# Seven-product blocks in all four feed-forward stages, and a changed supply of their weights

## The chip, the cores and the metric

The kernel runs on one NeuronCore of a Trainium2 chip, as one program. The metric is the device time of one execution in microseconds. The engines are TensorE (PE, with its weight loads PEld), VectorE (DVE), ScalarE (ACT), GpSimd (POOL) and SyncE (SP), which issues all DMAs of the kernel before.

## The reference

A sequence of 512 tokens with 1024 channels, all in fp32, goes through two blocks. The first has two layers; each is a feed-forward stage, a token mixing (three kinds of attention) and a second feed-forward stage, so there are four of these (`D_FF` is 2816):

```python
def swiglu(h, w_gate, w_up, w_down):
    return (jax.nn.silu(h @ w_gate) * (h @ w_up)) @ w_down
...
for l in range(DEPTH):
    x = x + 0.5 * swiglu(rmsnorm(x, ffn1_norm[l]), ffn1_w_gate[l], ffn1_w_up[l], ffn1_w_down[l])
    x = x + token_mixing(rmsnorm(x, mix_norm[l]), ...)
    x = x + 0.5 * swiglu(rmsnorm(x, ffn2_norm[l]), ffn2_w_gate[l], ffn2_w_up[l], ffn2_w_down[l])
```

The second block projects the normed x with one wide matrix, runs a state-space scan (S5) and a gated recurrence (RG-LRU) over the sequence, and merges the two.

## The kernel before, in words

**Layout.** Activations are held transposed: `xt[m]`, m from 0 to 7, is [128 channels, 512 tokens]. To keep fp32 accuracy each matmul operand is split into a high part in fp32r and a low part, the rest; `mm3` (L170) makes three matmuls, high by high, high by low and low by high. `wload` (L155) fetches a weight tile of up to [128, 1024] to a raw tile (tag `raw`, three buffers) by a DMA on SP's queue. For each piece of 512 columns ScalarE copies the high part (L164) and VectorE subtracts for the low part (L165), into the tags `whi` and `wlo`, four buffers each. `split` (L175) does the same for other operands.

**Stages 0 and 3, `ffn` (L227).** The 2816 hidden features are 22 rows of 128. A row needs two weight tiles, gate and up, of 24 matmuls with 512 columns each; I call each of these a row tile. Eleven rows are made, then their down products (L257) into the eight `xt[m]`; then the other eleven. A hook runs one step of side work for each row: `positions` (L420) in stage 0 makes the attention's bias tables and the rotary angles, `prepare` (L1001) in stage 3 makes block 2's constant operands. Both are generators, and most of their steps are VectorE work with some DMA writes. `prepare` also has transposes and small matmuls for each of its four parts.

**Stages 1 and 2, `ffn_blocks` (L319).** The first four rows (`NCLS` pairs) are row tiles as above. While they run, `blocks` (L330) norms x and makes from pairs of x tiles, halved in tokens, the seven operands of a Strassen-Winograd product; four are sums, kept in `ts` and split into `xh` and `xl` after the fourth row. Then each of nine pairs of rows makes two block problems, gate and up, with `gate_up` (L275): two raw tiles are fetched, VectorE makes four sums (L284 to L287), seven [128, 512] operands are split into pieces (ring of 8 from `whi` and `wlo`, and `NFX` = 12 from `fx`), and seven products of 12 matmuls with 256 columns accumulate in PSUM. ScalarE copies (L304, L306, L308) and VectorE adds (L310 to L315) take results out between them, where the next product goes on in the same bank:

```python
product(y, "a11", "b11", True)
act(c1[:, L], y, AF.Copy)
product(z, "s1", "t1", True)
act(c2[:, R], z, AF.Copy)
product(y, "s2", "t2", False)
act(c1[:, R], y, AF.Copy)
```

A problem has 84 matmuls with 256 columns in the place of two row tiles with 48 of 512. The pairs stand in groups, `FGRP` (L50), of 8, 8 and 6 rows, each followed by its down products (L406).

**Block 2, `block2` (L1158).** Its middle part runs four streams (L1384): the scan `s5`, the recurrence `lru`, the gates, and a final norm. Steps are interleaved by a list of due times. All of its projections fetch weights through `wload`, 32 tiles of 1024 columns and ten of 256 (L1301) in the streams. POOL has products of its own there (L1231, L1309, L1326).

**What sets the order.** The program is written in one order; a list scheduler then orders each engine's instructions by that order's priority and its estimate of when operands and buffers come free. An instruction may so run ahead of earlier ones on its engine if its buffers are free. A tile in a closed pool's space waits for the tiles that lay there.

Of the kernel before, what the change touches and what calls it, by code (L numbers as in the profile page):

```python
# [17 lines left out]
P = 128  # L18
# [31 lines left out]
FGRP = ((0, 8), (8, 16), (16, 22))  # L50
NCLS = 2
NFX = 12
BLOCKS = (1, 2)
# [46 lines left out]
def body(tc, A, out, tap, upto=99):  # L100
# [7 lines left out]
    with ctx:  # L108
# [45 lines left out]

        def wload(src, n):  # L155
# [71 lines left out]
        def ffn(i, nxt, pre, hook=None):  # L227
            with tc.tile_pool(name=f"fp{i}", bufs=1, reuse_waits="tile") as fp:
                for hf in range(2):
                    hh, hl = [], []  # L230
                    for f in range(NH):
                        ff = hf * NH + f
                        if hook is not None and ff >= 1:
                            if ff == 1:
                                work = hook(fp)
                            next(work, None)
                        gp = psum("pg")
                        up = psum("pu")
                        for j, o in ((0, gp), (1, up)):
                            wh, wl = ahead if i == ff == j == 0 else wload(A[f"gu{i}"][ff, :, j, :], KD * P)  # L240
                            for k in range(KD):
                                c = slice(k * P, (k + 1) * P)
                                mm3(o, wh[:, c], wl[:, c], xh[KORD[k]], xl[KORD[k]], k == 0, k == KD - 1)
                            if ff == 0:
                                next(pre)
                        t = tmp("t")
                        u = tmp("u")
                        V.tensor_tensor(t, gp, rstd, op=ALU.mult)
                        act(t, t, AF.Silu)
                        V.tensor_tensor(u, up, rstd, op=ALU.mult)  # L250
                        V.tensor_tensor(u, u, t, op=ALU.mult)
                        a = fp.tile([P, S], F32R, tag="h", name="hh", bufs=2 * NH)
                        b = fp.tile([P, S], F32R, tag="h", name="hl", bufs=2 * NH)
                        split(a, b, u)
                        hh.append(a)
                        hl.append(b)
                    for m in range(KD):  # L257
                        o = psum("pd")
                        for k0, k1 in ((0, 6), (6, NH)):
                            wh, wl = wload(A[f"dn{i}"][m][:, (hf * NH + k0) * P:(hf * NH + k1) * P], (k1 - k0) * P)  # L260
                            for k in range(k0, k1):
                                c = slice((k - k0) * P, (k - k0 + 1) * P)
                                mm3(o, wh[:, c], wl[:, c], hh[k], hl[k], k == 0, k == NH - 1)
                        V.scalar_tensor_tensor(out=xt[m], in0=o, scalar=0.5, in1=xt[m], op0=ALU.mult, op1=ALU.add)
                        if hf == 1 and nxt is not None:
                            nxt.tile(m)

# [7 lines left out]
        def gate_up(p, j, xk, fp, turn):  # L275

            rows = []
            for f in (2 * p, 2 * p + 1):
                r = wp.tile([P, WMAX], F32, tag="raw", name="raw", bufs=NRAW)
# [9 lines left out]
            for n, w in (("a11", a11), ("s1", s1), ("s2", s2), ("s4", s4), ("s3", s3), ("a12", a12), ("a22", a22)):  # L289
                ws[n] = piece(fp, turn), piece(fp, turn)  # L290
                split(*ws[n], w)
# [14 lines left out]
            act(c2[:, R], z, AF.Copy)  # L306
            product(y, "s2", "t2", False)
            act(c1[:, R], y, AF.Copy)  # L308
            product(z, "s4", "b22", False)
            V.tensor_tensor(c1[:, R], z, c1[:, R], op=ALU.add)  # L310
            product(y, "s3", "t3", False)
            V.tensor_tensor(c2[:, R], y, c2[:, R], op=ALU.add)
            x = psum("sx")[:, L]
            product(x, "a12", "b21", True)
            V.tensor_tensor(c1[:, L], x, c1[:, L], op=ALU.add)  # L315
            product(y, "a22", "t4", False)
            return c1, c2, y

        def ffn_blocks(i, nxt, pre):  # L319
            with tc.tile_pool(name=f"fp{i}", bufs=1, reuse_waits="tile") as fp:  # L320
                def htile(name, dt=F32R):
                    return fp.tile([P, S], dt, tag="h", name=name, bufs=16)
# [5 lines left out]
                ts = []  # L328

                def blocks(q):  # L330
                    xn = []
                    for m in (2 * q, 2 * q + 1):
                        t = htile("xn", F32)
                        V.scalar_tensor_tensor(out=t, in0=xt[m], scalar=vc(pre_gain, m), in1=rstd, op0=ALU.mult, op1=ALU.mult)
                        xn.append(t)
                    ta, tb = htile("ta", F32), htile("tb", F32)
# [7 lines left out]
                    ts.extend((ta, tb))  # L344
# [6 lines left out]
                pre_gain = pre[1]  # L351
                turn = [0]
                for g, (f0, f1) in enumerate(FGRP):
                    hh, hl = [], []

# [1271 lines left out]
```

## Time and profile before

| | us |
|---|---|
| median of 3 runs | 2672.49 (2671.57 to 2672.68) |
| profiled execution, own time | 2671.1 |
| its span in the trace | 2669.3 |
| TensorE busy | 2563.2 |
| VectorE busy | 1852.2 |
| ScalarE busy | 1290.5 |
| POOL busy | 108.9 |

Busy time is the union of an engine's instructions, not its peak. In the rows below a window's line gives its length, then the busy time of PE, PEld, DVE, ACT and POOL, each with the number of instructions that touch the window, then the granted TensorE clock as a share of 2.4 GHz and the DMA engines' share and GB/s. A line of a group gives count, busy time, mean of one in ns, and the idle time before them with what ended it.

### The profile page before, as it was taken

To read this page: it belongs to the slowest core of one execution; us is meant where nothing else is said; L and a number is where in the kernel's file an instruction comes from. 1 tells how busy PE (TensorE), PEld (TensorE's weight loads), DVE (VectorE), ACT (ScalarE), POOL (GpSimd) and SP (SyncE) were. 2 spreads that over 40 slices of the span, in tenths; PEclk is the share of its full clock that TensorE was granted. 3 is DMA by queue.
4 is the path that set the end of the run, shared out by engine and by line. 5 is a ranking of instruction groups with operands and counts; after the bars stand their busy time and mean duration, and the time that the engine had idled before them with its cause. 6 is when DMAs were issued, how large, how long until landed. Compare 5 with 4: busy or idle time off the path is not lost.

```text
span 2669.3 us, 36064 instructions
## 1 busy us (share of the span) xinstructions
PE 2563.2 (96%) x13140; PEld 2132.9 (80%) x13140; DVE 1852.2 (69%) x3533; ACT 1290.5 (48%) x2382; POOL 108.9 (4%) x113
## 2 busy tenths in 40 slices
PE   8999999999999999899999999999999978889998
PEld 6888888777789998889888877788888767668885
DVE  8634457888777586867676888766464699994435
ACT  5423346656445454535355666543343454563342
POOL 0000000000000000000000000000000013210001
PEclk9999999999999999999999999999999989989998
DMA  7432245763233332232335575233342444323332
GB/s 236 135 102 95 89 148 176 223 200 91 96 103 103 95 105 93 79 104 95 111 107 186 172 237 146 93 134 124 124 152 84 154 143 140 123 75 123 102 107 91
DMA packets 124354, 340.12 MB, mean 127 GB/s; under 512 B 17296, under 2 KB 25488, under 8 KB 123664
## 3 DMA queue, kind: packets, MB, share of 16 engines
q1 hardware_dynamic: 124176, 337.82, 40.1%
q8 instruction: 103, 1.69, 0.3%
q14 instruction: 75, 0.61, 0.1%
HBM read 279.56 MB, written 51.90 MB: 124 GB/s over the span
## 4 chain that ended last, share of the span: by engine, by line
PE 79%; DVE 14%; DMA 3%; ACT 2%; issue 2%; POOL 0%; POOLq 0%; SPq 0%; DVEq 0%; ACTq 0%
PE pd L172 6%; PE pd L171 6%; PE pd L173 6%; PE pg L171 4%; PE pg L172 4%; PE pg L173 4%; PE pu L171 3%; PE pu L172 3%; PE pu L173 3%; PE s L554 2%; PE sy L171 2%; DMA raw<-in_gu 2%; PE sy L173 2%; PE sy L172 2%; PE tp L583 1%
## 5 line engine op out<-in xcount | busy, mean ns | idle before, releaser
L164 ACT ACTIVATE whi<-raw 128x512 fp32r<-128x512 f32 (+1 forms) x738 | 431.8, 590 | 782.0 <-PE pd L172 237.9
L165 DVE TENSOR_TENSOR wlo<-raw,whi 128x512 fp32r<-128x512 f32 (+1 forms) x738 | 475.1, 649 | 366.9 <-ACT whi L164 319.4
L172 PE MATMUL pd<-hl,whi 128*128 128x512 f32 x704 | 278.1, 395 | 0.0
L173 PE MATMUL pd<-hh,wlo 128*128 128x512 f32 x704 | 278.1, 395 | 0.0
L171 PE MATMUL pd<-hh,whi 128*128 128x512 f32 x704 | 278.0, 395 | 0.0
L171 PE MATMUL pg<-xh,whi 128*128 128x512 f32 x480 | 192.4, 401 | 7.7 <-ACT xh L211 7.7
L172 PE MATMUL pg<-xl,whi 128*128 128x512 f32 x480 | 191.0, 398 | 0.3 <-DVE xl L212 0.3
L173 PE MATMUL pg<-xh,wlo 128*128 128x512 f32 x480 | 190.6, 397 | 0.0
L173 PEld LDWEIGHTS pd<-hh,wlo 128*128 128x128 f32 x704 | 132.0, 187 | 32.2
L171 PEld LDWEIGHTS pd<-hh,whi 128*128 128x128 f32 x704 | 132.0, 187 | 32.1
L172 PEld LDWEIGHTS pd<-hl,whi 128*128 128x128 f32 x704 | 132.0, 187 | 32.0
L171 PE MATMUL pu<-xh,whi 128*128 128x512 f32 x384 | 152.3, 397 | 0.0
L172 PE MATMUL pu<-xl,whi 128*128 128x512 f32 x384 | 151.6, 395 | 0.0
L173 PE MATMUL pu<-xh,wlo 128*128 128x512 f32 x384 | 151.3, 394 | 0.0
L171 PE MATMUL sy<-xh,wsp 128*128 128x256 f32 x432 | 123.0, 285 | 5.4 <-ACT c L304 4.2
L176 ACT ACTIVATE wsp<-fs 128x512 fp32r<-128x512 f32 x144 | 88.1, 627 | 70.3 <-DVE fs L284 43.1
L172 PE MATMUL sy<-xl,wsp 128*128 128x256 f32 x432 | 121.2, 280 | 0.0
L173 PE MATMUL sy<-xh,wsp 128*128 128x256 f32 x432 | 121.1, 280 | 0.0
L171 PEld LDWEIGHTS pg<-xh,whi 128*128 128x128 f32 x480 | 90.9, 189 | 29.9 <-ACT xh L211 8.7
L172 PEld LDWEIGHTS pg<-xl,whi 128*128 128x128 f32 x480 | 90.7, 189 | 23.4 <-DVE xl L212 2.2
L173 PEld LDWEIGHTS pg<-xh,wlo 128*128 128x128 f32 x480 | 90.8, 189 | 22.3
L177 DVE TENSOR_TENSOR wsp<-fs,wsp 128x512 fp32r<-128x512 f32 x144 | 92.2, 685 | 6.0 <-ACT wsp L176 5.6
(629 smaller groups left out, 6471.4 us busy)
## 6 DMA issues: line engine op xcount, KB each, us to landing
raw<-in_gu SPq DMA_DIRECT2D x176, 512.0 KB, 3.6
raw<-in_w SPq DMA_DIRECT2D x44, 512.0 KB, 3.7
raw<-in_dn SPq DMA_DIRECT2D x48, 384.0 KB, 3.2
b<-bias SPq DMA_DIRECT2D x64, 256.0 KB, 4.0
raw<-in_dn SPq DMA_DIRECT2D x32, 512.0 KB, 3.6
raw<-in_wf SPq DMA_DIRECT2D x28, 512.0 KB, 4.4
raw<-in_dn SPq DMA_DIRECT2D x32, 320.0 KB, 2.9
raw<-in_wo SPq DMA_DIRECT2D x16, 512.0 KB, 3.7
```

Source lines behind the costliest of these rows:

```text
L164: act(hi[:, :w], r, AF.Copy)
L165: weng[0].tensor_tensor(lo[:, :w], r, hi[:, :w].bitcast(F32), op=ALU.subtract)
L171: nc.tensor.matmul(o, wh, ah, start=first, stop=False, skip_group_check=more)
L172: nc.tensor.matmul(o, wh, al, start=False, stop=False, skip_group_check=more)
L173: nc.tensor.matmul(o, wl, ah, start=False, stop=last, skip_group_check=more)
L176: act(dst_h, src, AF.Copy)
L177: eng.tensor_tensor(dst_l, src, dst_h.bitcast(F32), op=ALU.subtract)
L554: nc.tensor.matmul(sps, a[:, c], b, start=i == 0, stop=i == len(passes) - 1)
L583: nc.tensor.transpose(tp[:, k * P:(k + 1) * P], e[:, k * P:(k + 1) * P], ident)
```

## The change

- All four feed-forward stages run one `ffn`: four rows as row tiles, then 18 block problems. The groups become 6, 6, 6 and 4 rows, with 12 buffers for hidden tiles instead of 16.
- `gate_up` is cut in two: `blocks_of` fetches, sums and splits; `gate_up` makes the products and yields between them. The last two products of a problem are issued among the first of the next one: a11, s1, (a12 before), s2, (a22 before), s4, s3.
- Raw weights for the problems rotate over six tiles, three of `raw` and three of a new tag; the ring of pieces has 8 + 10.
- The blocks' work tiles live in a pool for each group (`fw`), closed before the group's down products; a pool for side work (`fq`) takes the space during them.
- At the entry, the first problem's `blocks_of` stands ahead of the splits of the eight sums, and the hidden tiles of rows 2 and 3 are finished after those.
- Side work moves from the row tiles into the down products: `positions` to stage 0 (4, 4 and 2 steps behind the first three groups), `prepare` to stage 1 (3, 4, 0, 4) and stage 2 (0, 4, 0, 4). Its tiles are fetched again or have fewer buffers where the space is shorter.
- Low parts in `wload` can be made otherwise (`weng[0]` None): ScalarE writes the negated high part, and a DMA issued by POOL adds the raw tile to it. This holds for rows 1 to 3 of each stage (12 pieces of 512 columns a stage) and for block 2's streams (64 of 512 columns, ten of 256).

The diff, cut to its core:

```diff
-FGRP = ((0, 8), (8, 16), (16, 22))
+FGRP = ((0, 6), (6, 12), (12, 18), (18, 22))
-NFX = 12
-BLOCKS = (1, 2)
+NFX = 10
+NFR = 3
...
+        def lowpart(lo, r, hi, by_dma):
+            if by_dma:
+                act(lo, r, AF.Copy, scale=-1.0)
+                G.dma_start(out=lo.bitcast(F32), in_=r, accum_op=ALU.add)
+            else:
+                V.tensor_tensor(lo, r, hi.bitcast(F32), op=ALU.subtract)
...
-                weng[0].tensor_tensor(lo[:, :w], r, hi[:, :w].bitcast(F32), op=ALU.subtract)
+                lowpart(lo[:, :w], r, hi[:, :w], weng[0] is None)
...
+                n = turn[1] % (NRAW + NFR)
+                turn[1] += 1
+                if n < NRAW:
+                    r = wp.tile([P, WMAX], F32, tag="raw", name="raw", bufs=NRAW)
+                else:
+                    r = fp.tile([P, WMAX], F32, tag="fr", name="raw", bufs=NFR)
...
+                us = []
+                for f in range(2 * NCLS):
+                    us.append(rows(f))
+                    if f < 2:
+                        finish(us.pop())
                 for g, (f0, f1) in enumerate(FGRP):
+                    with tc.tile_pool(name=f"fw{i}{g}", bufs=1, reuse_waits="tile") as fw:
+                        turn = [0, 0]
+                        last, end = None, None
+                        for p in range(max(f0 // 2, NCLS), f1 // 2):
+                            for j in range(2):
+                                ws = blocks_of(p, j, xk, fw, turn)
+                                if p == NCLS and j == 0:
+                                    for m, t in enumerate(ts):
+                                        split(xh[m], xl[m], t)
+                                    while us:
+                                        finish(us.pop(0))
+                                cur = gate_up(ws, xk)
+                                next(cur)
+                                if last:
+                                    next(last)
+                                next(cur)
+                                if last:
+                                    end(*next(last))
+                                next(cur)
+                                last, end = cur, (gate, up)[j]
+                        next(last)
+                        end(*next(last))
                     n = f1 - f0
+                    with tc.tile_pool(name=f"fq{i}{g}", bufs=1, reuse_waits="tile") as fq:
+                        late.pool = fq
+                        done = 0
...
+                            while done < steps[g] * (m + 1) / KD:
+                                next(work, None)
+                                done += 1
...
+                        weng[0] = V if f == 0 else None
+                        wh, wl = ahead if i == f == j == 0 else wload(W[f, :, j, :], KD * P)
+                        weng[0] = V
...
         def block2(pre):
+            weng[0] = None
...
+                weng[0] = V
                 with tc.tile_pool(name="bd", bufs=1, reuse_waits="tile") as bd:
...
-                    if 2 * l in BLOCKS:
-                        ffn_blocks(2 * l, nrm, (cur.done(), f"ffn1_norm{l}"))
-                    else:
-                        ffn(2 * l, nrm, cur.done(), positions if l == 0 else None)
+                    ffn(2 * l, nrm, cur.done(), f"ffn1_norm{l}", side[l], ((4, 4, 2, 0), (0, 4, 0, 4))[l])
...
+                    ffn(2 * l + 1, nrm, cur.done(), f"ffn2_norm{l}", side[1], ((3, 4, 0, 4), (0, 0, 0, 0))[l])
```

## Rows read from the trace of the kernel before

**Rows 1.** The page, parts 1 and 4: busy share by engine, chain by engine

```profile
PE 2563.2 (96%) x13140; PEld 2132.9 (80%) x13140; DVE 1852.2 (69%) x3533; ACT 1290.5 (48%) x2382; POOL 108.9 (4%) x113
...
PE 79%; DVE 14%; DMA 3%; ACT 2%; issue 2%; POOL 0%; POOLq 0%; SPq 0%; DVEq 0%; ACTq 0%
```

**Rows 2.** Windows by stage: length, busy (count) by engine, clock, DMA share, GB/s

```profile
0.00:383.40 383.40, 375.47 (x1596) 300.18 (x1597) 212.66 (x470) 148.11 (x255) 1.83 (x7) 1.00 0.41 132
...
684.30:1042.80 358.50, 352.05 (x2246) 317.95 (x2245) 262.41 (x458) 176.03 (x332) 1.01 (x1) 0.99 0.30 97
1042.80:1408.90 366.10, 354.55 (x2245) 318.35 (x2244) 262.42 (x458) 173.68 (x330) 1.01 (x1) 0.99 0.32 100
...
1710.60:2092.20 381.60, 381.60 (x1694) 308.98 (x1693) 230.72 (x543) 158.38 (x278) 5.25 (x13) 1.00 0.37 121
2092.20:2376.10 283.90, 242.65 (x1045) 189.94 (x1044) 259.90 (x428) 148.06 (x220) 62.91 (x65) 0.92 0.40 130
```

**Rows 3.** Windows: row tiles, entries, groups of blocks, down products

```profile
198.60:321.80 123.20, 123.20 (x529) 99.11 (x529) 56.82 (x87) 40.90 (x65) 0.00 (x0) 1.00 0.28 90
730.40:778.90 48.50, 42.31 (x338) 41.66 (x337) 42.06 (x74) 26.46 (x55) 0.00 (x0) 0.93 0.31 104
778.90:823.70 44.80, 44.80 (x195) 36.00 (x194) 22.52 (x36) 13.46 (x23) 0.00 (x0) 1.00 0.27 88
823.70:904.10 80.40, 80.17 (x674) 79.93 (x673) 66.03 (x120) 46.27 (x94) 0.00 (x0) 1.00 0.31 100
...
1088.90:1139.60 50.70, 43.17 (x338) 41.86 (x337) 42.15 (x74) 26.29 (x55) 0.00 (x0) 0.93 0.32 98
...
1184.40:1268.60 84.20, 81.27 (x674) 80.11 (x673) 66.01 (x120) 45.68 (x94) 0.00 (x0) 1.00 0.30 96
...
1313.40:1375.30 61.90, 60.80 (x505) 60.12 (x504) 46.94 (x85) 33.13 (x69) 0.00 (x0) 1.00 0.28 88
1375.30:1408.90 33.60, 33.60 (x146) 27.00 (x145) 23.64 (x38) 18.18 (x31) 0.00 (x0) 1.00 0.50 158
```

**Rows 4.** PE's waits in stage 2: total us, times, longest us

```profile
PE sy L173 <- DVE wsp L177: 5.4, 1, 5.4
PE sy L171 <- ACT c L304: 4.0, 7, 1.4
```

**Rows 5.** Timeline of DVE in a group of stage 2: start, us, [idle before]

```profile
1238.29 0.69 DVE L284 TENSOR_TENSOR fs<-raw 128x512 f32<-128x512 f32 x1 [2.88 <-DMA raw<-in_gu]
```

**Rows 6.** Timeline of DVE around the end of down products

```profile
815.26 0.68 DVE L287 TENSOR_TENSOR fs<-fs,raw 128x512 f32<-128x512 f32 x1
...
824.09 0.68 DVE L412 SCALAR_TENSOR_TENSOR xt<-pd,xt 128x512 f32<-128x512 f32 x1
```

**Rows 7.** Lines of DVE, 0 to 200: busy us, mean ns

```profile
L165 DVE TENSOR_TENSOR wlo<-raw,whi 128x512 fp32r<-128x512 f32 x64 | 43.9, 687 | 44.8 <-ACT whi L164 27.2 <-PE pd L172 17.6
L447 DVE SCALAR_TENSOR_TENSOR ba<-d,lnc 128x512 f32<-128x512 f32 x16 | 11.0, 686 | 0.3 <-DMA bias<-bc 0.2 <-DMA lnc<-in_lnc 0.2
```

**Rows 8.** Window: row tiles of stage 3 beside preparation steps

```profile
1740.00:1841.00 101.00, 101.00 (x460) 82.21 (x459) 72.41 (x189) 46.14 (x80) 2.11 (x4) 1.00 0.41 140
```

**Rows 9.** Lines of DVE and ACT, 2092.2 to 2376.1

```profile
L165 DVE TENSOR_TENSOR wlo<-raw,whi 128x512 fp32r<-128x512 f32 x64 | 48.7, 777 | 9.5 <-ACT whi L164 7.3 <-PE pb L201 2.1
L164 ACT ACTIVATE whi<-raw 128x512 fp32r<-128x512 f32 x64 | 39.5, 625 | 62.1 <-PE plx L172 11.0 <-PE pgl L172 9.9 <-DMA raw<-in_w 9.7
...
L165 DVE TENSOR_TENSOR wlo<-raw,whi 128x256 fp32r<-128x256 f32 x10 | 5.3, 533 | 0.5 <-ACT whi L164 0.5
```

**Rows 10.** Lines of POOL, 2092.2 to 2376.1

```profile
L1231 POOL TENSOR_TENSOR m<-m,tb 128x512 f32<-128x512 f32 x16 | 30.2, 1886 | 75.1 <-DVE m L1219 44.9 <-issue 30.2
...
L980 POOL TENSOR_TENSOR colb<-colb,mhalf 128x4 f32<-128x4 f32 x1 | 1.0, 1007 | 160.4 <-DVE colb L979 160.4
```

**Rows 11.** DMA issues: KB each, median us to landing

```profile
gd<-g SPq DMA_DIRECT2D x8, 256.0 KB, 2.0
...
x<-x SPq DMA_DIRECT2D x8, 256.0 KB, 4.7
```

More of the change, by code (lines that the diff above doesn't have):

```diff
@@ L225, in done @@
                 yield col
[L227 to L266, printed above, removed]
         def piece(fp, turn):
@@ L312, in gate_up @@
             V.tensor_tensor(c2[:, R], y, c2[:, R], op=ALU.add)
+            yield
             x = psum("sx")[:, L]
@@ L315, in gate_up, with tile, ffn @@
             V.tensor_tensor(c1[:, L], x, c1[:, L], op=ALU.add)
+            yield
             product(y, "a22", "t4", False)
-            return c1, c2, y
-        def ffn_blocks(i, nxt, pre):
+            yield c1, c2, y
+        class Side:
+            def tile(self, *a, **k):
+                return self.pool.tile(*a, **k)
+        def ffn(i, nxt, pre, gain, work, steps):
             with tc.tile_pool(name=f"fp{i}", bufs=1, reuse_waits="tile") as fp:
                 def htile(name, dt=F32R):
-                    return fp.tile([P, S], dt, tag="h", name=name, bufs=16)
+                    return fp.tile([P, S], dt, tag="h", name=name, bufs=12)
                 L, R = slice(0, 256), slice(256, 512)
@@ new lines, in ffn, with finish, rows @@
+                hh, hl = [], []
+                def finish(u):
+                    a, b = htile("hh"), htile("hl")
+                    split(a, b, u)
+                    hh.append(a)
+                    hl.append(b)
+                def rows(f):
+                    o = [None, None]
+                    for j in range(2):
+                        o[j] = psum("pg")
+                        weng[0] = V if f == 0 else None
+                        wh, wl = ahead if i == f == j == 0 else wload(W[f, :, j, :], KD * P)
+                        weng[0] = V
+                        for k in range(KD):
+                            c = slice(k * P, (k + 1) * P)
+                            mm3(o[j], wh[:, c], wl[:, c], xh[KORD[k]], xl[KORD[k]], k == 0, k == KD - 1)
+                        if f == 0:
+                            next(pre)
+                        elif todo:
+                            blocks(todo.pop(0))
+                    t, u = tmp("t"), tmp("u")
+                    V.tensor_tensor(t, o[0], rstd, op=ALU.mult)
+                    act(t, t, AF.Silu)
+                    V.tensor_tensor(u, o[1], rstd, op=ALU.mult)
+                    V.tensor_tensor(u, u, t, op=ALU.mult)
+                    return u
@@ L1002, in tmp @@
             def tmp(name):
-                return fp.tile([P, S], F32, tag="pz", name=name, bufs=6)
+                return fp.tile([P, S], F32, tag="pz", name=name, bufs=5)
             def softplus():
@@ L1073, in prepare @@
             yield
-            kk = fp.tile([P, 256], F32, tag="kk", name="kk")
-            dma(kk, A["kk"])
             def cmul(dr_, di_, xr, xi, yr, yi):
@@ L1087, in prepare @@
             for ct in range(4):
+                kk = fp.tile([P, 256], F32, tag="kk", name="kk")
+                dma(kk, A["kk"])
                 g4 = slice(4 * ct, 4 * ct + 4)
@@ L1517, in body @@
                 bias_d = dp.tile([8, 4, P, S], F32, tag="bias", name="bias")
+                late = Side()
+                side = positions(late), prepare(late)
                 for l in range(DEPTH):
```

129 lines of the change are left out of this document (49 added, 80 removed).

## The prediction, with its working

> **What bounds the kernel now.** I read the page's busy shares and its chain first, then the sums by stage, then inside the stages.
> TensorE is busy for 2563.2 of 2669.3 us, and its matmuls are 79% of the chain, VectorE's work 14% [rows 1]. So what removes matmul time counts almost in full, except in a stage where VectorE leads.
> The sums by stage show which stage is which [rows 2]. The two old-style feed-forward stages (0: 0 to 383.4, 3: 1710.6 to 2092.2) have TensorE busy throughout. The two with seven-product blocks (1 and 2) take 358.5 and 366.1 us, 6.5 and 11.5 us of it without a matmul. The stretch from 2092.2 to 2376.1, where block 2's streams run, is another thing: VectorE is busy for 259.9 of 283.9 us, TensorE for 242.7, and the granted clock is down to 0.92. There VectorE sets the pace.
>
> **The change, part by part.** The sum is made against the profiled execution's span, 2669.3 us; its own time is 2671.1 us, 1.4 below the median 2672.49.
>
> *1. Blocks in stages 0 and 3.* 22 row tiles took 123.2 us, 5.60 each; eight block problems took 80.4 us, 10.05 each [rows 3]. A problem replaces two row tiles (one of gate or up for two rows), so it saves 11.20 - 10.05 = 1.15 us. Nine pairs by two make 18 problems a stage, and two stages turn: 36 x 1.15 = **-41.4 us**. The down products are the same in number, only cut in four groups instead of two.
>
> *2. What stages 1 and 2 lose today.* Against 10.05 us a problem, the entries lose 48.5 - 40.2 = 8.3 and 50.7 - 40.2 = 10.5 us, and two later groups of stage 2 lose 84.2 - 80.4 = 3.8 and 61.9 - 60.3 = 1.6 [rows 3]: 24.2 us. The entry's loss is TensorE waiting for the first low part, 5.4 us in one piece, and then for copies out of PSUM [rows 4]; VectorE had the eight sums' low parts queued ahead. The later losses begin where VectorE waits 2.88 us for raw weights, with three raw tiles [rows 5]. The change doubles the raw tiles, puts the first problem's parts ahead of the sums in program order, takes 12 low parts of 0.69 us a stage from VectorE, and puts other products between a copy and the bank's next use. So the 24.2 us are counted as removed (**-24.2**), and the new schedule is charged anew:
> - entry, four stages: between 0 and today's 9.4 us each; I take 3, as the causes shrink but the sums' own low parts stay. **+12.0**
> - steady problems, 72: the smaller pool of 18 pieces lets the parts of the first two products start only four and three products (1.44 us each) ahead, instead of nine. Between 0 and 0.5 us a problem (stage 2's 3.8 us over eight is the nearest loss); VectorE is busy 66.0 of 80.4 us, so it has room, and I take 0.1. **+7.2**
>
> *3. Group changes and side work.* Today the next group's sums run on VectorE before the last residual addition of the down products [rows 6], so a change of group costs nothing. Where the freed space is reused for side work, they must wait for it.
> - Tables of positions (stage 0, after groups 0, 1 and 2): four steps are eight additions of 0.686 us [rows 7], eight scalings and two distances, some 11 us at most, beside a down stretch of 18 x 8 matmuls, 33.6 us, in which VectorE has under 17 us of its own (22.5 of 44.8 in the group of eight [rows 3]). It fits, with the new start's 7 us; I charge 1.5 each for writes still in flight, **+4.5** (0 to 4 us each). Their DMA writes move on SP's queue from the row tiles to the down products, where the weight loads behind them have 2 tiles in hand.
> - Preparation for block 2: a 101 us row stretch of stage 3 with two groups of its steps has 72.4 us of VectorE [rows 8] against 56.8 in a plain 123.2, or 46.6 in 101 [rows 3]: 13 us for four steps. Behind group 1 of stages 1 and 2, 17 + 13 + 7 us of work against 33.6: **+8.0** for both. Behind the last group, the stretch is only 8 x 12 x 0.233 = 22.4 us. VectorE does 23.6 us in today's 33.6 [rows 3], about 20 with single weight pieces; with 13 more it is 11 us late for the next stage's inputs. Between 0 and 11 each; I take 6: **+12.0**. The preparation's own matmuls are the same ones, moved.
> - The other changes of group: seven at 0.3, **+2.0**.
>
> *4. Low parts by an accumulating DMA.* In block 2's streams 64 + 10 low parts, 48.7 + 5.3 = 54.0 us of VectorE, go [rows 9]. ScalarE gets as many negated copies, some 44 us by the high parts' row (39.5 for 64), and has 148.1 of 283.9 us busy. POOL issues 74 transfers. VectorE would have 259.9 - 54.0 = 205.9 us, ScalarE 191.7, TensorE its 242.7. So the gain lies between 0 and 283.9 - 242.7 = 41.2 us (a loss is priced below). I take two thirds, **-28.0**: three engines in one chain of dependences, though VectorE alone is packed to 92% today.
> The trace shows no such transfer and no DMA issued by POOL. Its chain: copy 0.63, negated copy 0.63, an issue (between nothing and a POOL product's 1.89; I take the 1.0 of POOL's smallest product [rows 10]), and the transfer: 256 KB took 2.0 and 4.7 us to land [rows 11], and with the destination read too between 2 and 9.4; I take 5. That is 7.3 us. The ring of four pieces holds two row tiles: a piece is used for 2.8 us of every 11.2, so 8.4 us are free. In the row tiles it is therefore hidden by 1.1 us, and costs nothing; without that cover each microsecond over 8.4 costs half a microsecond a tile.
> What could speak against the move shows in the rows: the same low part takes VectorE 687 ns in stage 0 and 777 in block 2, where POOL multiplies [rows 7, 9]. The Trainium skill ("SBUF — State Buffer", section "Who interferes with whom") says that the two engines lock a shared port pair: a POOL instruction that reads collides with VectorE's two-input ones, and a DMA issued by POOL can starve while VectorE copies in two-port modes. By that page's rule the 74 issues would write descriptors, not read, and the two-input subtractions around them would not be slowed; the sum stays as above. No run here shows POOL issuing yet. The same skill's "DMA: Bandwidth & Descriptors" (section "Anatomy of one DMA — SWDGE (gpsimd) path") gives 2.0 us plus bytes by 436 GB/s, an estimate of 2.6 us for 256 KB, which would leave the cover at 3.5 us.
>
> **Sum:** -41.4 - 24.2 + 12.0 + 7.2 + 4.5 + 8.0 + 12.0 + 2.0 - 28.0 = **-47.9 us**, a span of 2621.4 us, or 2624.6 against the median: **2624 us**.
>
> **Rivals.**
> *A. POOL is the new brake in block 2.* If each issue holds POOL 1.0 us and VectorE for as long, 74 us come back against 54 saved, at least on the two-input half: 37 us back, 17 left, and the chain's length eats those. For: 777 against 687 ns, and POOL's products wait in order for ScalarE. Then part 4 gives 0: 2624 + 28 = 2652 us.
> *B. Nothing new stalls.* Side work and parts are pulled ahead wherever there is room, as the rows of a down stretch show [rows 6]; entry, side work and steady losses vanish and block 2 becomes TensorE's: -41.4 - 24.2 - 41.2 = -106.8, 2566 us. Against: VectorE at 82% in the blocks with shorter leads.
> *C. Slower: the accumulating transfer is late everywhere.* Its place is the ring of two weight tiles; a tile then takes half of (chain + 2.8). There are 24 such tiles in the row stretches (5.60 us each now) and 32 in block 2 (8.9 of stretch each now, 283.9 / 32). Besides part 4, the change brings -19.9. Break-even: 24 (y - 5.6) + 32 (y - 8.9) = 19.9, y = 7.84, a chain of 12.9 us. From there it decides; at 16 us, y = 9.4 and the time is 2672.5 - 19.9 + 91.2 + 16.0 = 2760. For: POOL and ScalarE serve in order, and POOL's 16 products alone stand 75.1 us in wait now [rows 10]. Against: 7.3 by the nearest rows, and none of the rows' transfers is near 10.
> *D. The short leads and the shared space cost their bounds* (entry 9.4, 0.5 a problem): 25.6 + 28.8 over the sum, 2678 us, no gain worth the name.
>
> **How the numbers follow.** Forecast (2595 to 2640) 0.47; A 0.20; B 0.17; C 0.06; D 0.06; between or beyond these 0.04. The range takes in B and most of A and of D's way: 2566 to 2668, leaving out C, D and the far side of B. About 0.2% (5.3 us) is what a measurement of this kernel can tell from no change: faster by more 0.86 (all but C, D and a little of A), within it 0.05, slower 0.09.
>
> **What would show it.** Right: stages 0 and 3 near 372 and 357 us with 18 x 84 block matmuls each; problems at 10.05 to 10.2 us; TensorE's wait for the first low part under 4 us at each of the four entries; no wait for raw weights inside a group; in block 2 VectorE near 206 us and the stretch near 256. Wrong: matmuls waiting for the accumulating transfers in the second to fourth row of a stage or in block 2's projections (C); POOL busy or waiting ahead of its issues while VectorE's two-input operations pass 800 ns (A); waits at the start of each group after side work, or before the mixing's first matmul, of more than 6 us (part 3).

## The result and the profile after

The changed kernel takes 2634.02 us (median of four runs, 2632.25 to 2639.02), the kernel before 2672.59 in the same comparison: a ratio of 0.9858, 95% interval 0.9841 to 0.9875. It is faster by 38.6 us; 47.9 were forecast. The profiled execution's span is 2630.5 us, 38.8 below the one before.

The page of the changed kernel: the busy shares, then by engine the chain, that is the work that ended last, followed back step by step to what released it:

```profile
PE 2517.6 (96%) x14436; PEld 2163.0 (82%) x14436; DVE 1994.3 (76%) x3853; ACT 1450.3 (55%) x2765; POOL 209.7 (8%) x235
...
PE 79%; DVE 12%; DMA 3%; issue 3%; ACT 2%; POOL 1%; SPq 0%; POOLq 0%; DVEq 0%; ACTq 0%
```

Against [rows 1], TensorE has more matmuls and is busy 45.6 us less, VectorE is busy 142 us more. The windows of the changed kernel by stage (stages 0 to 3, then block 2's streams), answering to [rows 2]:

```profile
0.00:367.60 367.60, 356.05 (x2244) 318.55 (x2245) 307.81 (x668) 199.20 (x387) 12.36 (x19) 1.00 0.48 149
...
667.90:1037.90 370.00, 360.48 (x2294) 323.96 (x2293) 287.00 (x589) 196.65 (x377) 13.44 (x17) 0.99 0.39 116
1037.90:1408.90 371.00, 360.99 (x2294) 323.74 (x2293) 289.81 (x595) 196.68 (x380) 13.40 (x17) 0.99 0.41 124
...
1710.30:2063.80 353.50, 351.02 (x2246) 317.12 (x2245) 261.17 (x462) 187.75 (x359) 13.02 (x19) 1.00 0.38 108
2063.80:2339.10 275.30, 236.36 (x1046) 185.22 (x1045) 223.49 (x361) 182.13 (x295) 120.45 (x142) 0.94 0.80 200
```

| part | before | after | difference | forecast |
|---|---|---|---|---|
| stage 0 | 383.4 | 367.6 | -15.8 | |
| stage 1 | 358.5 | 370.0 | +11.5 | |
| stage 2 | 366.1 | 371.0 | +4.9 | |
| stage 3 | 381.6 | 353.5 | -28.1 | |
| four stages | 1489.6 | 1462.1 | -27.5 | -19.9 |
| block 2's streams | 283.9 | 275.3 | -8.6 | -28.0 |
| the rest (span less these) | 895.8 | 893.1 | -2.7 | 0 |

So the stages gave 7.6 us more than forecast, and the streams 19.4 less. Part of the shift between stages is work that moved: the preparation's 96 matmuls and transposes stand in stages 1 and 2 now, 48 in each (x2246 to x2294, x2245 to x2293). Inside the stages, the windows of the changed kernel that answer to [rows 3]: stage 1's entry, its plain down products, a group of six problems, the down products with preparation behind group 1 and behind the last group, stage 2's last down products, and stage 3's entry.

```profile
714.00:738.70 24.70, 22.18 (x170) 21.53 (x169) 20.61 (x38) 14.82 (x31) 0.00 (x0) 0.93 0.22 62
738.70:772.40 33.70, 33.70 (x147) 27.10 (x146) 19.41 (x34) 11.03 (x21) 0.00 (x0) 1.00 0.44 141
772.40:832.30 59.90, 59.90 (x506) 59.90 (x505) 50.34 (x91) 35.57 (x72) 0.99 (x2) 1.00 0.27 83
832.30:869.30 37.00, 36.42 (x170) 29.55 (x169) 30.41 (x92) 17.33 (x32) 0.00 (x0) 1.00 0.48 163
1002.90:1037.90 35.00, 28.83 (x123) 22.04 (x122) 31.48 (x92) 19.71 (x36) 0.00 (x0) 0.90 0.34 118
...
1372.40:1408.90 36.50, 30.32 (x123) 23.37 (x122) 31.41 (x92) 19.80 (x36) 0.00 (x0) 0.86 0.45 160
1756.30:1780.90 24.60, 22.12 (x169) 21.43 (x168) 21.22 (x39) 15.35 (x32) 0.00 (x0) 0.93 0.23 65
```

A problem takes 59.9 / 6 = 9.98 us with TensorE busy throughout. The preparation behind group 1 lengthens the down products by 3.3 us, 2.7 of which are its own matmuls (busy 36.42 against 33.70). Behind the last group, whose plain down products take 22.5 us (stage 3, 2041.1 to 2063.7), the same work makes 35.0 and 36.5 us, with the granted clock down to 0.90 and 0.86. TensorE's waits in stage 1, which answer to [rows 4], name the cause (the first and the third line; the second is the entry's): VectorE, busy 31.5 of 35.0 us there, is late with the down weights' low parts and with the preparation's own operands.

```profile
PE pd L180 <- DVE wlo L160: 3.5, 2, 2.0
PE sy L178 <- ACT c L278: 2.7, 2, 2.5
PE zt L1136 <- DVE z L1133: 2.5, 2, 1.4
```

In block 2's streams the DMA engines' share has doubled from 0.40 to 0.80, and the low parts cost nearly as much engine time as all other transfers. The DMA view of the stretch 2063.8 to 2339.1 (queue: packets, MB, share of 16 engines; then KB each and us from issue to landing):

```profile
q1 hardware_dynamic: 14426, 37.08, 41.6%
q0 software_dynamic: 10512, 17.83, 38.1%
...
wlo<-raw POOLq DMA_DIRECT2D x63, 256.0 KB, 4.7
```

### The profile page after: what moved, and what is told of

It is laid out like the page before. It is cut to its first block, busy times and chain, and to the rows that moved or that the text cites. A ratio compares the mean times of both kernels' runs of the same rounds, so it can differ in the third digit from the quotient of the medians.

```text
span 2630.5 us, 39897 instructions
## 1 busy us (share of the span) xinstructions
PE 2517.6 (96%) x14436; PEld 2163.0 (82%) x14436; DVE 1994.3 (76%) x3853; ACT 1450.3 (55%) x2765; POOL 209.7 (8%) x235
## 4 chain that ended last, share of the span: by engine, by line
PE 79%; DVE 12%; DMA 3%; issue 3%; ACT 2%; POOL 1%; SPq 0%; POOLq 0%; DVEq 0%; ACTq 0%
PE pd L180 5%; PE sy L178 5%; PE sy L180 5%; PE sy L179 5%; PE pd L178 5%; PE pd L179 5%; PE sz L179 3%; PE sz L180 2%; PE sz L178 2%; PE pg L180 2%; PE pg L179 2%; PE pg L178 2%; PE s L573 2%; PE tp L602 1%; PE sx L178 1%
## 5 line engine op out<-in xcount | busy, mean ns | idle before, releaser
L171 ACT ACTIVATE whi<-raw 128x512 fp32r<-128x512 f32 (+1 forms) x594 | 341.1, 580 | 551.9 <-PE pd L179 184.1
L160 DVE TENSOR_TENSOR wlo<-raw,whi 128x512 fp32r<-128x512 f32 (+2 forms) x472 | 288.2, 617 | 240.9 <-ACT whi L171 234.9
L178 PE MATMUL sy<-xh,wsp 128*128 128x256 f32 x864 | 243.3, 282 | 9.4 <-ACT c L278 9.4
L179 PE MATMUL sy<-xl,wsp 128*128 128x256 f32 x864 | 243.8, 282 | 0.0
L180 PE MATMUL sy<-xh,wsp 128*128 128x256 f32 x864 | 243.2, 281 | 0.0
L184 DVE TENSOR_TENSOR wsp<-fs,wsp 128x512 fp32r<-128x512 f32 x288 | 190.8, 684 | 15.1 <-ACT wsp L183 12.9
L183 ACT ACTIVATE wsp<-raw 128x512 fp32r<-128x512 f32 x216 | 133.3, 627 | 91.7 <-PE sy L179 37.1
L178 PEld LDWEIGHTS sy<-xh,wsp 128*128 128x128 f32 x864 | 164.0, 190 | 10.6 <-ACT c L278 10.6
L158 POOL DMA_DIRECT2D wlo<-raw x122 | 106.9, 906 | 792.3 <-ACT wlo L157 754.5
L180 PEld LDWEIGHTS pd<-hh,wlo 128*128 128x128 f32 x704 | 133.0, 189 | 41.4 <-DVE wlo L160 9.3
L179 PEld LDWEIGHTS sy<-xl,wsp 128*128 128x128 f32 x864 | 162.9, 189 | 0.6 <-DVE xl L184 0.6
L180 PEld LDWEIGHTS sy<-xh,wsp 128*128 128x128 f32 x864 | 163.3, 189 | 0.0
L184 DVE TENSOR_TENSOR wsp<-raw,wsp 128x512 fp32r<-128x512 f32 x216 | 146.3, 683 | 8.5 <-ACT wsp L183 8.2
L418 DVE SCALAR_TENSOR_TENSOR xt<-pd,xt 128x512 f32<-128x512 f32 x128 | 88.1, 689 | 26.1 <-PE pd L180 25.3
```

The lines of the kernel that those rows point to most:

```text
L158: G.dma_start(out=lo.bitcast(F32), in_=r, accum_op=ALU.add)
L160: V.tensor_tensor(lo, r, hi.bitcast(F32), op=ALU.subtract)
L178: nc.tensor.matmul(o, wh, ah, start=first, stop=False, skip_group_check=more)
L179: nc.tensor.matmul(o, wh, al, start=False, stop=False, skip_group_check=more)
L180: nc.tensor.matmul(o, wl, ah, start=False, stop=last, skip_group_check=more)
L183: act(dst_h, src, AF.Copy)
```

## The experiments

Block 2's numbers are read from the streams' own stretch in each profile. Five of the kernels here have the same program in it (the changed one and runs 4 to 7): their streams take 272.9 to 275.3 us, and the entry that run 3 singles out 21.6 to 24.4. The other stages vary by up to 5 us from one profile to the next with the same program in them (stage 2: 371.0 us in the changed kernel, 375.4 and 375.8 in the first and third run below), and that may be in the medians too.

**1. All low parts of block 2 on VectorE.**

```diff
         def block2(pre):
-            weng[0] = None
+            weng[0] = V
```

> Only the low parts of block 2's streams go back to VectorE; the feed-forward stages stay as changed. Changed kernel: 2634.0 us, its streams 275.3 us (2063.8 to 2339.1) against 283.9 before. Theory 1, the DMA engines became the bound there (their share went from 0.40 to 0.80, the accumulating queue alone 0.38 for 17.8 MB): the move is worth its 8.6 us, so 2641 to 2645 us, DMA share back near 0.40, VectorE back near 260 us busy. Theory 2, POOL's issues only slow VectorE by as much as they spare it: the same 2641 to 2645, but then the second and third run tell. Rival, the 8.6 us came from something else (another place of the side work, another schedule): 2634 within 2 us.

2653.04 us (ratio to the kernel before 0.9928, 0.9912 to 0.9944). The streams take 289.6 us: the transfers are worth 14.3 us inside this kernel, not 8.6. These streams are 5.7 longer than those before, with the same work and 0.90 against 0.92 of the clock. For some 235 us the two keep within 1.2 us of each other, and the difference comes up behind that, mostly as TensorE waiting longer; why it waits longer there stays open. The profiled run was the slowest of four (2657.0), so part may be spread.

**2. Half the columns each way** (first 512 of each tile on VectorE, the rest by transfer).

```diff
-                lowpart(lo[:, :w], r, hi[:, :w], weng[0] is None)
+                lowpart(lo[:, :w], r, hi[:, :w], weng[0] is None or weng[0] == 1 and i > 0)
...
-            weng[0] = None
+            weng[0] = 1
```

> In block 2's streams the first 512 columns of a weight tile get their low part from VectorE again, the second 512 by the accumulating DMA: 32 instead of 74 such transfers. Theory 1 (DMA engines saturated at 0.80): DMA share near 0.60, VectorE near 245 us, and a stretch shorter than both 275.3 and 283.9: 262 to 270 us, so 2621 to 2629 us. Theory 2 (POOL slows VectorE by what it spares): gains and costs both halve, the stretch lies between, 277 to 281 us, 2636 to 2640.

2646.26 us (0.9901, 0.9884 to 0.9918), streams 282.3: halfway between the two pure forms (275.3 and 289.6). That is the second theory's rule, though its numbers, made with the 283.9 of before, miss; the first falls, and there is no optimum in the middle.

**3. The same transfers with an eighth of the bytes.** Only the first 64 of 512 columns are accumulated, so a part of each low part is left out of the sums.

```diff
-                G.dma_start(out=lo.bitcast(F32), in_=r, accum_op=ALU.add)
+                G.dma_start(out=lo[:, :64].bitcast(F32), in_=r[:, :64], accum_op=ALU.add)
```

(in block 2 alone)

> As the changed kernel, but each accumulating DMA of block 2's streams adds only the first 64 of its columns (a quarter or an eighth of the bytes, the same 128 rows); the other columns of those low parts are left as the negated high part, so this part of the sum is left out. ScalarE's copies and POOL's 74 issues stay. Theory 1 (bytes on the DMA engines are the bound): DMA share from 0.80 to about 0.50, the transfers land in under 3.5 us instead of 4.7, and the stretch falls towards my predicted 256 us: 252 to 264, 2611 to 2623 us. Theory 2 (POOL's issues and the port shared with VectorE): no change, 272 to 277 us, 2631 to 2636, VectorE's slowed operations (1248 ns at L1251) as slow as before.

2630.04 us (0.9836, 0.9814 to 0.9857), streams 264.0. The median fits the second theory, but its stages 1 and 2 and the mixing behind them were 9.0 us longer in its profile than in the changed kernel's; the streams, 11.3 us shorter, fit the first, as do the DMA engines' share (0.53) and the landing (2.9 us at the median); VectorE's slowed product stays slow (1220 ns), as the second has it. 289.6 - 264.0 = 25.6 us is what VectorE's relief is worth inside this kernel when the transfers are light, 19.9 us against the streams before; 28 were forecast. 11.3 us of it is given back with the whole bytes.

Where it is given back shows when the streams are cut where the fourth projection (`pgm`) begins: the entry, then the rest. Before, the first run and the third run:

```profile
2092.20:2111.00 18.80, 18.80 (x92) 15.47 (x91) 7.86 (x17) 5.76 (x10) 1.98 (x2) 1.00 0.60 224
2111.00:2376.10 265.10, 223.85 (x955) 174.47 (x954) 252.05 (x411) 142.30 (x211) 60.93 (x63) 0.91 0.39 123
```

```profile
2072.20:2091.10 18.90, 18.90 (x93) 15.58 (x92) 10.45 (x22) 7.54 (x13) 2.34 (x2) 1.00 0.64 224
2091.10:2361.80 270.70, 225.41 (x956) 175.70 (x955) 252.40 (x411) 142.49 (x212) 59.92 (x63) 0.89 0.37 121
```

```profile
2072.10:2091.10 19.00, 19.00 (x94) 15.63 (x92) 5.62 (x14) 10.60 (x20) 8.51 (x14) 1.00 0.75 230
2091.10:2336.10 245.00, 214.96 (x955) 169.91 (x954) 214.53 (x347) 171.93 (x277) 113.76 (x128) 0.94 0.52 143
```

And the changed kernel, with VectorE's longest wait in the stretch and the first long piece of its chain:

```profile
2063.80:2088.20 24.40, 20.83 (x93) 16.44 (x91) 5.45 (x13) 10.47 (x19) 8.30 (x14) 0.93 0.91 242
2088.20:2339.00 250.80, 215.43 (x955) 168.71 (x954) 217.94 (x348) 171.62 (x276) 112.15 (x128) 0.94 0.79 196
```

```profile
DVE u L1201 <- ACT rstd L209: 15.9, 1, 15.9
```

```profile
2068.62 9.63 DMA wlo<-raw
```

The entry alone loses 24.4 - 19.0 = 5.4 us: a transfer of 9.63 us, twice the median, stands on the chain, and VectorE waits 15.9 us with nothing to do. TensorE stands still for 3.6 us of the 24.4; the rest of the loss is the same matmuls at a lower granted clock (busy 20.83 us at 0.93, 19.00 at 1.00).

**4. Side work one group earlier.**

```diff
-                    ffn(2 * l, nrm, cur.done(), f"ffn1_norm{l}", side[l], ((4, 4, 2, 0), (0, 4, 0, 4))[l])
+                    ffn(2 * l, nrm, cur.done(), f"ffn1_norm{l}", side[l], ((4, 4, 2, 0), (0, 4, 4, 0))[l])
...
-                    ffn(2 * l + 1, nrm, cur.done(), f"ffn2_norm{l}", side[1], ((3, 4, 0, 4), (0, 0, 0, 0))[l])
+                    ffn(2 * l + 1, nrm, cur.done(), f"ffn2_norm{l}", side[1], ((3, 4, 4, 0), (0, 0, 0, 0))[l])
```

> The preparation's four steps behind the last group of stages 1 and 2 (4 rows, 22.4 us of down products, which took 35.1 and 36.6 us) move behind the third group (6 rows, 33.6 us). Theory: VectorE is short there by some 10 us, once in each stage, since the norm of the next stage stands in the same stretch; behind a group of 6 rows the same steps cost 37.0 instead of 33.7 us, matmuls of their own 2.7 included. So each stage gains 35.8 - 22.5 - 3.4, 8 to 10 us, and the kernel 14 to 20: 2614 to 2620 us. Rival, the steps are as costly wherever they stand: within 3 us of 2634.

2615.15 us (0.9785, 0.9769 to 0.9801), as expected, about 19 us below the changed kernel. Stages 1 and 2 of this run:

```profile
671.40:1032.60 361.20, 356.68 (x2289) 321.94 (x2288) 288.92 (x593) 198.38 (x379) 13.41 (x17) 1.00 0.41 124
1032.60:1394.90 362.30, 358.17 (x2299) 323.39 (x2298) 291.09 (x596) 197.27 (x379) 13.39 (x17) 1.00 0.42 126
```

8.8 and 8.7 us less than with the work behind the last group, the last down products back at 22.5 us each, the granted clock at 1.00. The work is the same; a stretch of 33.6 us holds it, one of 22.5 does not.

**5. Stage 3 as row tiles again.** The core of the edit:

```diff
+                            if i == 3:
+                                while us:
+                                    finish(us.pop(0))
+                                for f in (2 * p, 2 * p + 1):
+                                    finish(rows(f))
+                                continue
                             for j in range(2):
                                 ws = blocks_of(p, j, xk, fw, turn)
```

> Base: the changed kernel (2634.0 us). Edit: stage 3 alone goes back to plain row tiles for all 22 rows (its weights' low parts for rows 1 to 3 still by transfer, the later rows' on VectorE), in the same four groups. Theory 1 (a problem is worth 11.20 - 10.05 us): 18 x 1.15 = 20.7 us back, less the entry's 4.5 us, +16: 2650, stage 3 at 370 us. Rival (stage 3 gained by the smaller groups and by the low parts that left VectorE, not by the products): stage 3 stays within 3 us of 353.5, 2632 to 2637.

2651.84 us (0.9916, 0.9894 to 0.9938). The stage takes 371.1 us, 17.6 more than with blocks:

```profile
1716.50:2087.60 371.10, 371.10 (x1598) 298.35 (x1597) 169.46 (x269) 134.75 (x226) 13.29 (x19) 1.00 0.36 102
```

The first theory holds: the gain is the products'. Against the 381.6 us of before, this stage has the smaller groups but not the preparation's 96 matmuls (x1598, x1694 before); TensorE is busy throughout both, so the 10.5 us between them are those matmuls, which moved, and the smaller groups give nothing by themselves.

**6. No overlap of block problems.**

```diff
-                                next(cur)
-                                if last:
-                                    next(last)
-                                next(cur)
-                                if last:
-                                    end(*next(last))
-                                next(cur)
-                                last, end = cur, (gate, up)[j]
-                        next(last)
-                        end(*next(last))
+                                for _ in range(4):
+                                    next(cur)
+                                (gate, up)[j](*next(cur))
```

> Base: the changed kernel (2634.0 us). Edit: in the feed-forward stages each problem's seven products and its end are issued before the next problem's first; nothing else changes. Theory 1 (the overlap pays for the smaller pool and keeps the waits for copies out of PSUM off the path): each of 72 problems loses 0.2 to 0.6 us, 14 to 43 us together: 2648 to 2677. Theory 2 (what the entries and problems lost before was the queue of low parts and the raw tiles alone): within 5 us of the changed kernel, 2630 to 2640.

2633.50 us (0.9858, 0.9836 to 0.9880): the same as with it. In its trace the products do stand one problem after the other, and a group of six problems takes 59.90 us either way:

```profile
772.30:832.20 59.90, 59.90 (x506) 59.90 (x505) 50.41 (x91) 35.41 (x72) 0.00 (x0) 1.00 0.28 83
```

The second theory holds. The overlap written into the program is worth nothing here.

**7. Three raw tiles in the blocks.**

```diff
-NFR = 3
+NFR = 0
```

> Base: the changed kernel (2634.0 us). Edit: three raw weight tiles instead of six in the blocks. Theory 1 (the raw weights arrived late with three, as in the stage before that lost 3.8 and 1.6 us in two groups): 1.5 to 5 us a stage in four stages, 2640 to 2654, with VectorE's waits for raw weights of 2 to 3 us back inside the groups. Theory 2 (the pool of pieces holds the parts back anyway, so the raw tiles have time): no change, 2630 to 2638.

2669.65 us (0.9983, 0.9972 to 0.9994): 35.6 us are gone, more than either theory had. VectorE's waits for raw weights over the whole span, first in this run, then in the changed kernel:

```profile
DVE fs L255 <- DMA raw<-in_gu: 92.2, 52, 4.6
```

```profile
DVE fs L255 <- DMA raw<-in_gu: 18.0, 8, 4.6
```

52 waits against 8, and the 8 stand at the starts of groups. The kernel before, with three raw tiles in its two stages of blocks, had 21 such waits of 26.1 us in all. The first group of stage 2 takes 65.5 us in place of 59.9, and the stages are 8.9, 9.0, 11.6 and 9.7 us longer. So without its three added raw tiles the change would lose almost its whole net gain; what six raw tiles would give the kernel before was not tried.

**8 to 10. A longer ring for block 2's weight pieces, and the low part ahead of the high part.** The base is run 4. The ring's core, then the order's:

```diff
-                hi = wp.tile([P, WP], F32R, tag="whi", name="whi", bufs=NWT)
-                lo = wp.tile([P, WP], F32R, tag="wlo", name="wlo", bufs=NWT)
+                hi, lo = held_piece("whi", NXH), held_piece("wlo", NXL)
...
+                if weng[0] is None:
+                    lowpart(lo[:, :w], r, None, True)
                 act(hi[:, :w], r, AF.Copy)
-                lowpart(lo[:, :w], r, hi[:, :w], weng[0] is None)
+                if weng[0] is not None:
+                    lowpart(lo[:, :w], r, hi[:, :w], False)
```

> Base: the kernel with the preparation's steps behind the third group (2615.15 us, block 2's streams 274.4 us of it). Edit: in block 2 the ring of low parts has six pieces instead of four and that of high parts five. Theory 1 (the accumulating transfers land late because a tile's chain of two copies 0.6 us each, issue 0.93 and transfer 4.4 must fit into the time in which a piece of a short ring is free): the streams shorten by 5 to 10 us, to 264 to 269, TensorE's waits for the transfers (about 8 us on the matmuls there now) fall below 3, and the time is 2604 to 2610. Theory 2 (the cost is the sharing, of the transfer engines that are 80% busy or of the ports, whenever the transfers run): the ring changes nothing, 2613 to 2618.

> Same base. Edit: where the low part comes by transfer, ScalarE writes the negated copy and the transfer is issued ahead of the high part's copy, in the same ring of four. Theory 1 (chain too long for the ring): the transfer starts 0.6 us earlier for each of 73 pieces in block 2, worth 2 to 5 us, and nothing in the stages: 2610 to 2613. Theory 2 (sharing): nothing gained, and the first product, which needs the high part, waits 0.6 us longer where ScalarE is late now (3.9 us in all): 2615 to 2619.

> Same base, both edits. Theory 1: at most what the streams gained when the transfers carried an eighth of their bytes (264.0 us against 275.3), so 2602 to 2608, with the streams at 263 to 268. Theory 2: 2613 to 2619.

2620.32, 2615.92 and 2613.55 us (0.9811, 0.9783 and 0.9772, half widths 0.0015 to 0.0022); streams 275.3, 274.8 and 273.8 us against 274.4. All three lie within the spread of one program's streams, so the first theory falls. With the ring, TensorE waits 3.9 us for the transfers instead of 8.2, and the time is spent at other waits; its waits in the streams:

```profile
PE yp L185 <- ACT hs L190: 10.4, 3, 6.8
PE pb L215 <- DVE bc L212: 6.1, 1, 6.1
...
PE pu L187 <- DMA wlo<-raw: 2.7, 1, 2.7
PE plg L187 <- DMA wlo<-raw: 0.9, 1, 0.9
PE pgl L187 <- DMA wlo<-raw: 0.3, 1, 0.3
```

The entry stays long in all three: 23.9, 25.3 and 26.3 us to the fourth projection.

**11. The first four projections' low parts on VectorE, the rest by transfer.** The base is run 4.

```diff
         def block2(pre):
-            weng[0] = None
+            weng[0] = V
...
                     o4 = proj(37, "pgm")
+                    weng[0] = None
```

> Base: the kernel with the preparation's steps behind the third group (2615.15 us; streams 274.4 us, of which 24.2 pass until the fourth projection begins, against 18.9 with all low parts on VectorE). Edit: the low parts of block 2's first four projections go back to VectorE, which waits 15.6 us in one piece there now; the later ones stay transfers. Theory 1 (part of what block 2 did not gain is a stall at its start, where the first transfers stand behind ScalarE's other work and take up to 9.6 us): the fourth projection begins 18.5 to 20 us after the start, the streams take 268 to 270, the time is 2608 to 2611. Theory 2 (the lost time is paid evenly, wherever transfers share the engines or ports): 273 to 275, 2613 to 2617.

2603.67 us (0.9746, 0.9731 to 0.9761), the best of all. Entry and rest, first of run 4, then of this run:

```profile
2049.50:2073.70 24.20, 20.98 (x94) 16.56 (x92) 5.55 (x14) 10.62 (x20) 8.44 (x14) 0.93 0.93 247
2073.70:2324.00 250.30, 216.30 (x955) 168.89 (x953) 215.89 (x348) 171.65 (x276) 112.45 (x128) 0.94 0.80 197
```

```profile
2043.60:2062.50 18.90, 18.90 (x93) 15.57 (x91) 9.76 (x21) 8.05 (x14) 3.26 (x3) 1.00 0.64 226
2062.50:2308.70 246.20, 212.50 (x956) 165.98 (x955) 214.84 (x346) 171.54 (x276) 113.52 (x128) 0.95 0.80 198
```

The entry is whole again (18.9 us), and the streams take 265.1 us, 9.3 less than in run 4 (7.8 to 10.2 by the five kernels with the same streams), with the DMA engines at 0.80 behind the entry as before. So of the 11.3 us of run 3, 9.3 can be had with whole transfers for all the later tiles, and 5.3 of them are the start. That the rest is 4.1 us shorter too was not expected; its cause stays open.

**12. POOL's 16 products of the S5 stream on VectorE.** The base is run 11.

```diff
-                            G.tensor_tensor(m2, gg, sb, op=ALU.mult)
+                            V.tensor_tensor(m2, gg, sb, op=ALU.mult)
```

> Base: the run before (first four projections on VectorE). Edit: the 16 products of the S5 stream that POOL makes (1.69 us each) go to VectorE. Theory 1 (POOL and VectorE disturb each other: VectorE's own product of the pair takes 1.25 us beside POOL's, 0.69 at the least, and POOL's products and the issues of transfers stand in each other's way in one queue): VectorE gets 16 x 0.69 = 11 us more and 16 x 0.56 = 9 us back, POOL loses 27 us, and the streams get 0 to 6 us shorter than the run before. Theory 2 (VectorE sets the pace and the longer products are only its own waiting): the streams get 7 to 12 us longer.

2607.53 us (0.9750, 0.9729 to 0.9770): no difference from run 11 that its four runs (2598.85 to 2609.47) could show. The streams take 264.2 us, 0.9 less, inside the first theory's 0 to 6 and far from the second's +7 to +12:

```profile
2047.00:2311.20 264.20, 231.71 (x1046) 181.74 (x1045) 221.18 (x385) 179.56 (x290) 91.35 (x115) 0.95 0.80 203
```

VectorE's own product of the pair before the change, in the changed kernel, and both products in this run:

```profile
L1232 DVE TENSOR_TENSOR m<-m,tb 128x512 f32<-128x512 f32 x16 | 13.0, 812 | 0.0
```

```profile
L1251 DVE TENSOR_TENSOR m<-m,tb 128x512 f32<-128x512 f32 x16 | 20.0, 1248 | 0.1
```

```profile
L1250 DVE TENSOR_TENSOR m<-m,tb 128x512 f32<-128x512 f32 x16 | 11.3, 709 | 0.1
L1251 DVE TENSOR_TENSOR m<-m,tb 128x512 f32<-128x512 f32 x16 | 10.9, 678 | 0.0
```

Sixteen products cost VectorE 20.0 us beside POOL; it makes all 32 alone in 22.2.

## Why the prediction was nearly right, step by step

The time lies 10 us above the forecast of 2624, and part of that nearness is luck: inside the stages three charges were too high and two too low, the streams gained a third of what was forecast, and the misses partly cancel. Of the signs that were named for a right prediction, those of the stages came: stages 0 and 3 take 367.6 and 353.5 us, and TensorE waits 0.7 us at most for the first low parts of an entry. Those of block 2 did not: VectorE is busy 223.5 us instead of 206, and the stretch takes 275.3 instead of 256.

**Step 1, the blocks (-41.4).** Right. Stage 3 undone cost 17.6 us; by the prediction's terms 18 x 1.15 = 20.7 less the entry's 4.5 us measured is 16.2.

**Step 2, today's losses and the new schedule.** The steady loss was forecast at +7.2 and was none: 9.98 us a problem, 0.07 under the 10.05 taken from the rows before, which makes -5 over 72 problems. The entries take 25.7, 24.7, 22.4 and 24.6 us for two problems, 97.4 - 4 x 20.1 = 17.0 us against 12.0: in three of them TensorE still waits 2.5 us in one piece for a copy out of PSUM, with the granted clock at 0.93; in stage 2's it waits 1.5 us, at 1.00. The reasons given, however, had their weights wrong. The prediction spread the removed 24.2 us over raw tiles, program order, low parts and the overlap. Runs 6 and 7 part two of these: the overlap gives nothing, the raw tiles 35.6 us, more than all the losses of before. Four stages of blocks instead of two, and the smaller pool, may be why; no run parts them.

**Step 3, side work.** The total came near, the parts did not. Behind group 1, +8.0 was charged for both; apart from the preparation's matmuls it is 2 x (3.3 - 2.7) = 1.2, and the groups behind it take 60.3 and 60.6 us against 59.9. Tables of positions: +4.5 charged, while the groups behind them take 60.6 and 60.3 us. Behind the last group, +12.0 was charged, from bounds of 0 to 11 each; measured are 35.0 and 36.5 against 22.5, less 2.7 of matmuls each: 9.8 and 11.3, of which TensorE stands still for 6.2 each and the rest is matmuls at the lower granted clock. Run 4 gives back 17.5. It was the upper bound that held. VectorE's shortfall had been worked out right (11 us late); half of it was then taken to hide, and nothing hid it.

**Step 4, low parts by transfer (-28.0): the step that failed.** VectorE's relief alone comes near that (19.9 or 25.6 us in run 3, by which streams it is set against). The parts of the chain were sized well too: its 7.3 us had a transfer of 5 (4.7 measured; the other estimate, 2.6, was too low) and an issue of 1.0 (0.93 measured), and in the feed-forward stages no matmul waited for a transfer. What the term lacked is the start: the ring's cover of 8.4 us was reckoned for a running pipeline, and block 2 begins with an empty one. There a transfer takes up to 9.6 us and is issued behind ScalarE's work for the norm, with the DMA engines at 0.91, while VectorE stands idle. Run 11 shows that giving VectorE four tiles brings back 9.3 of the missing 19.4 us, 5.3 of them at the start. VectorE's 223.5 us in place of 205.9 is a second miss: 7.0 us of it are the slowed products. Run 11's 265.1 us are still 9.2 above the forecast's 255.9; the share of two thirds was a choice, and no run shows what those 9.2 us are.

**The rivals.** A was half there: two-input operations passed 800 ns, 1248 on average for the worst group, as it said. But an issue, which does take POOL 0.93 us, does not hold VectorE (the last section has the lines), POOL is busy 120.5 of 275.3 us, and taking 28 us of products from it (run 12) changes nothing: its products are no brake. B was nearly true of the steady problems only. C did not come: the transfers land in 4.7 us. D's half microsecond a problem was none.

**What stays open.** The 5.7 us between the first run's streams and those before; the 4.1 us that the rest of run 11 gained; the 9.2 us that its streams still lack; how the 35.6 us of run 7 divide between late loads and the smaller pool. Putting the stages' own low parts (rows 1 to 3) back to VectorE was not tried; what the trace shows is that no matmul waits for a transfer there, and one weight load for 0.3 us.

## What to carry to other kernels

Price a new pipeline twice: running, and at its start, where the engine that it relieves is idle and the engines that feed it are not; the best version here uses the old way for the first four tiles and the new one after. Work moved into a stretch is hidden only by what the stretch's busiest helper has left, and the worked-out shortfall should be charged in full. When several parts of a change serve the same end, undo them one by one: three 4 KB buffers a partition carried 35.6 us, the overlap of the problems none.

## What the runs showed of the hardware

- Accumulating transfers issued by POOL take 38.1% of the DMA engines' time for 17.83 MB, the plain ones 41.6% for 37.08 MB: 1.9 times as much per byte. With an eighth of the bytes in as many packets (10512) the share was 10.7%.
- Each issue takes POOL 0.93 us on average, 0.86 at the median (64.3 us busy for 73 in the streams).
- A product of POOL can slow VectorE's two-input product beside it; POOL's issue of a transfer does not. VectorE's took 812 ns on average before, when POOL's stood 75.1 us in wait [rows 10], 1248 in the changed kernel, and 678 and 709 with POOL's gone. The Trainium skill ("SBUF — State Buffer", section "Who interferes with whom") tells of a port pair that the two share; the trace agrees on the slowing of VectorE. The slowest in the changed kernel, beside two products of POOL:

```profile
2178.44 3.80 DVE L1251 TENSOR_TENSOR m<-m,tb 128x512 f32<-128x512 f32 x1
2178.81 1.62 POOL L1250 TENSOR_TENSOR m<-m,tb 128x512 f32<-128x512 f32 x1
2180.07 1.61 POOL L1345 TENSOR_TENSOR g<-g,e 128x512 f32<-128x512 f32 x1
```

In run 12 ten of the 32 products ran beside an issue and nothing else of POOL's. They took 660 to 684 ns, the 16 beside nothing 662 to 694. One of the ten, with the issue:

```profile
2239.69 0.68 DVE L1251 TENSOR_TENSOR m<-m,tb 128x512 f32<-128x512 f32 x1
2239.81 0.85 POOL L158 DMA_DIRECT2D wlo<-raw  x1 [2.37 <-ACT wlo L157]
```

- Where TensorE stalled, the granted clock of the window fell: 0.86 and 0.90 behind the last groups, 0.93 at three of the four block entries (stage 2's, with the shortest wait, kept 1.00) and at block 2's. Without the stalls behind the last groups (run 4) stages 1 and 2 had 1.00.
